# Reordering the input products of the mixers in a two-layer hybrid trunk: an SSD group, two GLA heads, the other SSD group, the other two GLA heads

## The chip, the cores and the metric

The kernel runs on one core of a Trainium2 chip. The metric is the device time in microseconds (us) of one execution. Engines are named as in the profile: PE is the matrix engine (TensorE) and PEld its weight loads, which overlap it; DVE is VectorE, ACT is ScalarE, POOL is GpSimd, SP is SyncE, whose queue carries all the DMAs of the main loop.

## The reference

A trunk of two layers over 512 tokens of width 1024, in float32. Each layer has a mixer and a convolutional feed-forward block (FFN). The mixer projects the normalised tokens once, splits the columns among three sequence mixers, and merges the three results with sigmoid gates:

```python
def mixer_layer(u, w_in, ...):
    proj = u @ w_in                      # 1024 -> all columns below
    (gq, gk, gv, ga, gg, mqk, mv, mi, mf, mo, sz, sxbc, sdt, gates) = jnp.split(proj, ...)
    o_gla = gla(heads(gq, 4), heads(gk, 4), heads(gv, 4), heads(log_a, 4))
    y_gla = group_rmsnorm(o_gla, gla_norm, 4) * jax.nn.silu(gg)
    ...                                  # mlstm: y_m
    xbc = jax.nn.silu(causal_dwconv(sxbc, ssd_conv_w, ssd_conv_b))
    sx, sb, sc = jnp.split(xbc, ...)     # 1024, 2 groups x 128, 2 groups x 128
    y = ssd(heads(sx, 16), dt, a_neg, heads(sb, 2), heads(sc, 2))
    y = (y + ssd_d[:, None] * xh) * jax.nn.silu(sz)
    y_s = group_rmsnorm(y, ssd_norm, 2)
    z = einsum(stack([y_gla, y_m, y_s]), w_branch)
    return sum(sigmoid(gates + gate_b) * z) @ w_out
```

The SSD mixer has two groups of 512 columns of x. Within a group everything depends only on that group's own B, C and x columns (`sb`, `sc`, four tiles of `sx`), up to the gate with `sz` and the root-mean-square norm over the group. The GLA mixer has four heads, each with its q and k (128 columns) and v (256 columns).

## The kernel before, in words

Activations are held transposed: 128 columns by 512 tokens is one tile. A product of one output tile takes 8 slices of the contraction, and each slice three matmuls of 128x128 by 128x512, since weights and activations are split into a high and a low part (`wh`, `wl`, `uh`, `ul`) and the product of the two low parts is left out: 24 matmuls on PE for one output tile, written to one of four PSUM banks called `acc`. For v the operands change places and four `acc` tiles of 512 columns make two heads (`units_tok`). The four other banks are called `m` and serve everything that is no product of a weight: transposes, the scans' small matmuls, states.

Weights come in 512 KB pieces (`raw`, three buffers) by SP's queue; ACT rounds a piece to its high part (`wh`), DVE subtracts to get the low one (`wl`), and two buffers of each hold what PE reads, in units of two output tiles. DVE takes a finished bank out (as `cx`, `gq`, `gk`, `sz` or `G`) and, for SSD, runs a convolution of four taps on it (`cc`).

The table `MIX` lists the columns of the input projection in the order in which they are multiplied, and `layer()` walks it in the same order, with a closure for each tile that says what to do with the bank. The order before is the small columns (`S`), the first SSD group (`sb`, `sc`, four of x), the second SSD group, two GLA heads (q, k, q, k and then four tiles of v), two more GLA heads, the eight `sz` tiles, then gates, branch products and the mLSTM. Numbered from 0, a layer's tiles are 0 to 12 for SSD, 13 to 28 for GLA, 29 to 36 for `sz`.

The sequence mixers run in the background, as generators in `bg`: after each unit of two output tiles `bg` advances each of them by one step, so that their matmuls come between products. `rows` makes the decay rows, `ssd_group(g)` the states and the outputs `sy[4g]` to `sy[4g+3]` of a group, `gla_head(h)` a head, `fin_s(g)` the norm of an SSD group. `bg.drain(condition)` steps the generators until the condition holds. A step of `ssd_group`, called a mix below, takes a pair of decay tiles `bc` and an `eb`, which SP fetches from a scratch in DRAM (`dr`) by three or four DMAs, lets DVE and ACT turn them into matrices, and has PE multiply them by `xd`, the transposed and scaled x. The order in which a group of instructions stands on each engine is chosen by a scheduler when the kernel is built, from the program's order and from priorities, so that moving a tile in `MIX` moves the rows of all the queues.

`fin_s(g)` waits for the last `sz` tile of its group, sums the squares over the columns on PE (`m<-cst,sq`), gets variance and inverse root on DVE in small steps (`svar`, `srt`, `sr`; the line that adds them up is L935), has PE spread the result over the partitions (`rr`, `m<-cst,sr`), and multiplies the four `y` tiles (L238), which are then the activations (`yh`, `yl`) of the first branch product.

Of the kernel before, what the change touches and what calls it, by code (L numbers as in the profile page):

```python
# [53 lines left out]
MIX = ["S"]  # L54
for _g in range(2):
    MIX += [("sxbc", 1024 + 128 * _g), ("sxbc", 1280 + 128 * _g)]
    MIX += [("sxbc", 512 * _g + 128 * _i) for _i in range(4)]
NSSD = len(MIX)

TOK = []  # L60
for _h in range(0, 4, 2):
    MIX += [("gq", 128 * _h), ("gk", 128 * _h), ("gq", 128 * _h + 128), ("gk", 128 * _h + 128)]
    TOK.append(len(MIX))
    MIX += [("gv", 256 * _h + 128 * _i) for _i in range(4)]
# [10 lines left out]
for _h in range(0, 4, 2):  # L75
    MIX += [("mqk", 128 * _h), ("mqk", 512 + 128 * _h), ("mqk", 128 * _h + 128), ("mqk", 640 + 128 * _h)]
    TOK.append(len(MIX))
    MIX += [("mv", 256 * _h + 128 * _i) for _i in range(4)]
# [55 lines left out]
class Kern:  # L134
    def __init__(self, ctx, tc, xT, w8, w11, par, wa, cst, out):
# [44 lines left out]
        for l in range(L):  # L180
            i = 0
            while i < NMIX:
                if i in TOK:
                    self.chunks += [(2, l * N8 + i, k, 2) for k in range(2)]
                    i += 4
                    continue
                n = 1 if i == NSSD - 1 else 2
                self.chunks.append((0, l * N8 + i, KT, n))
# [683 lines left out]
    def layer(self, l):  # L872
        nc = self.nc
        bg = self.bg
# [12 lines left out]
        full = lambda xs: all(x is not None for x in xs)  # L887
        u = self.u


        def evx(i, store, j):
            def ev(ps):
                store[j] = self.silu2(*self.conv(ps, 4, "scw", i, 12, "scb", i))
            return ev
        evs = [lambda ps: bg.add(self.rows(ps))]
        for g in range(2):
            evs += [evx(8 + g, self.sb, g), evx(10 + g, self.sc, g)]
            evs += [evx(4 * g + i, self.sx, 4 * g + i) for i in range(4)]
        bg.add(self.ssd_group(0))
        bg.add(self.ssd_group(1))  # L900
        for i in range(0, NSSD, 2):
            self.wide = i < WIDE
            self.units(u, evs[i:i + 2], boundary=(i == 0), mid=(self.norm_end, self.norm_rows_of_cols))


        for h in range(4):
            def evq(ps):
                self.gq[h] = self.t("gq")
                with self.tc.high_priority(EV_PRIO):
                    self.stt(self.gq[h], ps, 128.0 ** -0.5, self.rstd, ALU.mult, ALU.mult)  # L910

            def evk(ps):
                self.gk[h] = self.t("gk")
                self.first(self.gk[h], ps)
            self.units(u, [evq, evk])
            if h % 2:
                for i in (h - 1, h):
                    self.gv[i] = Blocks([self.v() for _ in range(2)])
                self.units_tok(u, lambda b, ps: self.evac_tok(b, ps, self.gv[h - 1:h + 1]))
        bg.drain(lambda: full(self.sy))  # L920


        rsum_g = self.t("rsg")
        bg.add(self.stagger([self.gla_head(h, rsum_g) for h in range(4)], GLA_LAG))
        sqs, ready, ys, done_s = [None, None], [], [], []

        def fin_s(g):
            while g not in ready:
                yield
            for _ in range(SQY):  # L930
                yield
            ps = self.mps()
            self.colsum(ps, 0, sqs[g])
            var, r = self.small([P, NB], "svar"), self.small([P, NB], "sr")
            nc.vector.tensor_scalar(var, ps[:, 0:NB], 1.0 / 512, 4 * EPS, op0=ALU.mult, op1=ALU.add)  # L935
            with self.tc.high_priority(EV_PRIO):
                self.rsqrt(r, var, self.small([P, NB], "srt"))
            yield
            rr = self.rows_of_cols(r)
            for j in range(4 * g, 4 * g + 4):  # L940
                y = self.sy[j]
                self.stt(y, y, self.col("sn", j), rr, ALU.mult, ALU.mult)
                ys.append(self.split_tile(y))
                self.sy[j] = None
                if j % 2:
                    yield
            if g == 1:
                done_s.append(ys)
        bg.add(fin_s(0))
        bg.add(fin_s(1))  # L950
        for g in range(2):
            for i in range(2):
                def evz(ps, j):
                    s = self.t("sz")
                    self.first(s, ps)
                    s = self.silu2(s)
                    y = self.sy[j]
                    self.mul(y, y, s)
                    q = self.t("sq")
                    self.act(q, y, AF.Square)  # L960
                    if sqs[g] is not None:
                        self.tt(q, q, sqs[g], ALU.add)
                    sqs[g] = q
                    if j % 4 == 3:
                        ready.append(g)
                j = 4 * g + 2 * i
                self.units(u, [lambda ps: evz(ps, j), lambda ps: evz(ps, j + 1)])
# [280 lines left out]
GLA_LAG = 2  # L1248
# [3 lines left out]
WIDE = 2  # L1252
# [97 lines left out]
```

## Time and profile before

| | |
|---|---|
| time, median of 3 runs | 2295.11 us (2294.96 to 2295.38) |
| the profiled execution | 2295.16 us, of which 2293.3 us are the span |
| PE busy | 2279.3 us, 99% of the span |
| PE weight loads | 1876.8 us, 82% |
| DVE busy | 1434.1 us, 63% |
| ACT busy | 902.7 us, 39% |

The time of the profiled execution is the span plus 1.9 us around it. A share of busy time is a mean over the span; the chain that ended last tells which engine's work the end depended on, and idle time of PE, by what ended it, tells how much of the span another order could give back.

### The profile page before, as it was taken

The numbers are of one execution on the slowest core, as the hardware profiler recorded it, in microseconds if no ns is written. First come the engines' busy times: TensorE is split into PE (matmuls) and PEld (weight loads), VectorE is DVE, ScalarE is ACT, GpSimd is POOL, SyncE is SP. The second block draws the span as 40 slices with busy tenths as digits, with TensorE's granted clock in tenths as the row PEclk, the third lists the DMA queues.
The fourth block names the chain that finished last, engine by engine and source line by source line (L and its number), as shares of the span: only waits on it lengthen the run. The fifth ranks groups of instructions, "written<-read, shape, count | busy, mean of one in ns | idle before, by whom it ended". The sixth has DMA issues, their size and how long they took to land.

```text
span 2293.3 us, 27258 instructions
## 1 busy us (share of the span) xinstructions
PE 2279.3 (99%) x10832; PEld 1876.8 (82%) x10832; DVE 1434.1 (63%) x2165; ACT 902.7 (39%) x1344; POOL 2.8 (0%) x22
## 2 busy tenths in 40 slices
PE   9999999999999999999999999999999999999998
PEld 6878888888888888888888788888888888888887
DVE  6966745474464587467579767345744645873774
ACT  6534632333333344234354346233333433442432
POOL 0000000000000000000000000000000000000000
PEclk9999999999999999999999999999999999999999
DMA  5253223332232333232323522232322343232222
GB/s 181 85 156 101 74 74 104 99 120 93 87 111 97 129 100 107 82 101 97 128 85 102 162 92 74 77 107 93 129 90 90 101 132 107 93 97 94 94 91 75
DMA packets 78911, 235.73 MB, mean 103 GB/s; under 512 B 8872, under 2 KB 12264, under 8 KB 78784
## 3 DMA queue, kind: packets, MB, share of 16 engines
q1 hardware_dynamic: 78784, 233.99, 31.7%
q8 instruction: 85, 1.39, 0.3%
q14 instruction: 42, 0.34, 0.1%
HBM read 229.55 MB, written 4.41 MB: 102 GB/s over the span
## 4 chain that ended last, share of the span: by engine, by line
PE 93%; DVE 4%; ACT 2%; issue 1%; DMA 1%; SPq 0%; DVEq 0%; ACTq 0%
PE acc L241 65%; PE m L241 27%; DVE cc L238 1%; PE m L244 1%; ACT la L229 1%; DVE wl L232 1%; DVE la L610 0%; DMA h<-in_xT 0%; DVE og L232 0%; DVE cx L232 0%; DMA dn<-ry 0%; ACT zg L229 0%; ACT cc L229 0%; DVE zg L238 0%; ACT wh L229 0%
## 5 line engine op out<-in xcount | busy, mean ns | idle before, releaser
L229 ACT ACTIVATE wh<-raw 128x1024 fp32r<-128x1024 f32 (+2 forms) x372 | 385.1, 1077 | 586.1 <-PE acc L241 250.9
L241 PE MATMUL acc<-uh,wh 128*128 128x512 f32 x1552 | 609.3, 393 | 2.0 <-DVE mo L232 1.0
L241 PE MATMUL acc<-uh,wl 128*128 128x512 f32 x1552 | 605.9, 391 | 0.4 <-DVE wl L232 0.3
L241 PE MATMUL acc<-ul,wh 128*128 128x512 f32 x1552 | 605.7, 390 | 0.1
L232 DVE TENSOR_TENSOR wl<-raw,wh 128x1024 fp32r<-128x1024 f32 (+2 forms) x372 | 453.2, 1250 | 154.4 <-ACT wh L229 154.0
L241 PEld LDWEIGHTS acc<-uh,wh 128*128 128x128 f32 x1552 | 291.4, 188 | 64.2 <-issue 2.7
L241 PEld LDWEIGHTS acc<-uh,wl 128*128 128x128 f32 x1552 | 291.4, 188 | 62.7 <-DVE wl L232 1.5
L241 PEld LDWEIGHTS acc<-ul,wh 128*128 128x128 f32 x1552 | 291.4, 188 | 61.6 <-DVE ul L238 1.6
L238 DVE SCALAR_TENSOR_TENSOR cc<-cx,par,cc 128x510 f32<-128x510 f32 (+2 forms) x296 | 217.6, 748 | 41.0 <-ACT cc L229 36.9
L241 PE MATMUL acc<-yl,wh 128*128 128x512 f32 x512 | 200.0, 391 | 0.0
L241 PE MATMUL acc<-yh,wl 128*128 128x512 f32 x512 | 199.7, 390 | 0.0
L241 PE MATMUL acc<-yh,wh 128*128 128x512 f32 x512 | 199.6, 392 | 0.0
L241 PE MATMUL m<-uh,wh 128*128 128x512 f32 x384 | 149.8, 390 | 1.2 <-ACT wh L229 1.2
L241 PE MATMUL m<-uh,wl 128*128 128x512 f32 x384 | 149.9, 390 | 0.0
L241 PE MATMUL m<-ul,wh 128*128 128x512 f32 x384 | 149.4, 389 | 0.0
L229 ACT ACTIVATE cc<-cx,par 128x512 f32<-128x512 f32 x128 | 102.8, 809 | 86.6 <-DVE cx L232 86.5
L241 PE MATMUL m<-ah,wl 128*128 128x512 f32 x308 | 120.0, 390 | 0.0
L241 PE MATMUL m<-al,wh 128*128 128x512 f32 x308 | 119.8, 389 | 0.0
L241 PE MATMUL m<-ah,wh 128*128 128x512 f32 x308 | 119.5, 389 | 0.0
L241 PEld LDWEIGHTS acc<-yh,wl 128*128 128x128 f32 x512 | 96.1, 188 | 20.5 <-issue 0.4
L241 PEld LDWEIGHTS acc<-yh,wh 128*128 128x128 f32 x512 | 96.1, 188 | 19.8 <-DVE gg L232 0.4
L241 PEld LDWEIGHTS acc<-yl,wh 128*128 128x128 f32 x512 | 96.2, 188 | 19.5
(204 smaller groups left out, 2653.3 us busy)
## 6 DMA issues: line engine op xcount, KB each, us to landing
raw<-in_w SPq DMA_DIRECT2D x336, 512.0 KB, 3.6
raw<-in_w SPq DMA_DIRECT2D x32, 704.0 KB, 4.0
bc<-dr SPq DMA_DIRECT2D x48, 256.0 KB, 3.6
h<-in_xT SPq DMA_DIRECT2D x16, 256.0 KB, 6.6
eb<-dr SPq DMA_DIRECT2D x32, 128.0 KB, 4.5
bc<-dn SPq DMA_DIRECT2D x16, 256.0 KB, 3.1
kept<-h SPq DMA_DIRECT2D x8, 256.0 KB, 2.0
h<-kept SPq DMA_DIRECT2D x8, 256.0 KB, 5.6
```

Of the source, the lines that this page charges most:

```text
L229: return self.nc.scalar.activation(out, in_, func, bias=bias, scale=scale)
L232: return self.nc.vector.tensor_tensor(out, a, b, op=op)
L238: return self.nc.vector.scalar_tensor_tensor(out, a, s, b, op0=op0, op1=op1)
L241: return self.nc.tensor.matmul(out, lhsT, rhs, start=start, stop=stop)
L244: return self.nc.tensor.transpose(out, x, self.ident)
```

## The change

The table now puts GLA heads 0 and 1 between the two SSD groups, and heads 2 and 3 behind the second. Numbered from 0 the order is `S`, first SSD group (tiles 0 to 6), GLA heads 0 and 1 (7 to 14), second SSD group (15 to 20), GLA heads 2 and 3 (21 to 28), then `sz` as before. Before the gates of the first SSD group only its own four outputs are waited for (`sy[:4]`); the second group's are waited for before its own gates, and the four GLA heads join the background there, two units (four `sz` tiles) later than before. `NSSD`, the number of tiles in the part that is chunked without the pairs, now is 7 and not 13. The matmuls, their number and the buffers are the same; no line of a mixer changes.

```diff
@@ -55,10 +55,11 @@
 for _g in range(2):
     MIX += [("sxbc", 1024 + 128 * _g), ("sxbc", 1280 + 128 * _g)]
     MIX += [("sxbc", 512 * _g + 128 * _i) for _i in range(4)]
-NSSD = len(MIX)
-
-TOK = []
-for _h in range(0, 4, 2):
+    if _g == 0:
+        NSSD = len(MIX)
+
+        TOK = []
+    _h = 2 * _g
     MIX += [("gq", 128 * _h), ("gk", 128 * _h), ("gq", 128 * _h + 128), ("gk", 128 * _h + 128)]
     TOK.append(len(MIX))
     MIX += [("gv", 256 * _h + 128 * _i) for _i in range(4)]
@@ -892,18 +893,22 @@
             def ev(ps):
                 store[j] = self.silu2(*self.conv(ps, 4, "scw", i, 12, "scb", i))
             return ev
-        evs = [lambda ps: bg.add(self.rows(ps))]
-        for g in range(2):
+        bg.add(self.ssd_group(0))
+        bg.add(self.ssd_group(1))
+
+        def ssd_proj(g):
+            evs = [] if g else [lambda ps: bg.add(self.rows(ps))]
             evs += [evx(8 + g, self.sb, g), evx(10 + g, self.sc, g)]
             evs += [evx(4 * g + i, self.sx, 4 * g + i) for i in range(4)]
-        bg.add(self.ssd_group(0))
-        bg.add(self.ssd_group(1))
-        for i in range(0, NSSD, 2):
-            self.wide = i < WIDE
-            self.units(u, evs[i:i + 2], boundary=(i == 0), mid=(self.norm_end, self.norm_rows_of_cols))
+            for i in range(0, len(evs), 2):
+                self.wide = g == 0 and i < WIDE
+                first = g == 0 and i == 0
+                self.units(u, evs[i:i + 2], boundary=first, mid=(self.norm_end, self.norm_rows_of_cols))
 
 
         for h in range(4):
+            if h % 2 == 0:
+                ssd_proj(h // 2)
             def evq(ps):
                 self.gq[h] = self.t("gq")
                 with self.tc.high_priority(EV_PRIO):
@@ -917,11 +922,10 @@
                 for i in (h - 1, h):
                     self.gv[i] = Blocks([self.v() for _ in range(2)])
                 self.units_tok(u, lambda b, ps: self.evac_tok(b, ps, self.gv[h - 1:h + 1]))
-        bg.drain(lambda: full(self.sy))
+        bg.drain(lambda: full(self.sy[:4]))
 
 
         rsum_g = self.t("rsg")
-        bg.add(self.stagger([self.gla_head(h, rsum_g) for h in range(4)], GLA_LAG))
         sqs, ready, ys, done_s = [None, None], [], [], []
 
         def fin_s(g):
@@ -949,6 +953,9 @@
         bg.add(fin_s(0))
         bg.add(fin_s(1))
         for g in range(2):
+            if g == 1:
+                bg.drain(lambda: full(self.sy[4:]))
+                bg.add(self.stagger([self.gla_head(h, rsum_g) for h in range(4)], GLA_LAG))
             for i in range(2):
                 def evz(ps, j):
                     s = self.t("sz")
```

Line numbers of the changed kernel are one higher from the table on; so L238 of before is L239 there, and L271 is L272.

On SP's queue in the first layer, where the last DMAs of the mixes stand among the weight pieces (`raw`), the order before has weight pieces between the two `bc` of one mix.

```order
L845 DMA eb_221_1393<-dr_674 64x512
L502 DMA bc_1494<-dr_674 128x512
L502 DMA bc_1502<-dr_674 128x512
L844 DMA eb_237_1510<-dr_674 64x512
L845 DMA eb_237_1510<-dr_674 64x512
L271 DMA raw_1698<-in_w 128x1024
L502 DMA bc_1513<-dr_674 128x512
L271 DMA raw_1728<-in_w 128x1024
L502 DMA bc_1521<-dr_674 128x512
L844 DMA eb_240_1529<-dr_674 64x512
L845 DMA eb_240_1529<-dr_674 64x512
L271 DMA raw_1762<-in_w 128x1024
```

In the changed kernel the four mixes of the second group come one after the other (`bc_1422`, `bc_1491`, `bc_1611`, `bc_1711`), and this is the stretch with the second and the third of them.

```order
L845 DMA eb_225_1438<-dr_655 64x512
L846 DMA eb_225_1438<-dr_655 64x512
L503 DMA bc_1491<-dr_655 128x512
L503 DMA bc_1499<-dr_655 128x512
L845 DMA eb_235_1507<-dr_655 64x512
L846 DMA eb_235_1507<-dr_655 64x512
L503 DMA bc_1611<-dr_655 128x512
L503 DMA bc_1619<-dr_655 128x512
L845 DMA eb_255_1627<-dr_655 64x512
L846 DMA eb_255_1627<-dr_655 64x512
L272 DMA raw_1709<-in_w 128x1024
L272 DMA raw_1760<-in_w 128x1024
```

So the mixes of the second group follow one another with nothing of the first group between them, and a weight piece, `raw_1709`, stands behind the first three of them on the queue.

On DVE, where the norm of the second SSD group (`svar` to the last `sr`) leads to the first branch product in the first layer, the order before has the small steps on end, with one `G` bank taken out near their end.

```order
L935 TENSOR_SCALAR svar_2379<-m_2374 128x4
L474 TENSOR_SCALAR sr_2380<-svar_2379 128x4
L232 TENSOR_TENSOR srt_2382<-svar_2379,sr_2380 128x4
L238 SCALAR_TENSOR_TENSOR srt_2382<-srt_2382,sr_2380 128x4
L238 SCALAR_TENSOR_TENSOR sr_2380<-srt_2382,sr_2380 128x4
L232 TENSOR_TENSOR srt_2382<-svar_2379,sr_2380 128x4
L238 SCALAR_TENSOR_TENSOR srt_2382<-srt_2382,sr_2380 128x4
L238 SCALAR_TENSOR_TENSOR sr_2380<-srt_2382,sr_2380 128x4
L232 TENSOR_TENSOR srt_2382<-svar_2379,sr_2380 128x4
L238 SCALAR_TENSOR_TENSOR srt_2382<-srt_2382,sr_2380 128x4
L232 TENSOR_TENSOR G_2458<-acc_2433,rstd_263 128x512
L238 SCALAR_TENSOR_TENSOR sr_2380<-srt_2382,sr_2380 128x4
```

The changed kernel has three `ge` multiplications and three `gnb` of GLA heads, and two weight splits (`wl`), between the small steps; the first rows of the chain, from `svar_2244` on, stand just before these.

```order
L233 TENSOR_TENSOR srt_2247<-svar_2244,sr_2245 128x4
L233 TENSOR_TENSOR ge_2195<-ge_2195,gk_690 128x384
L623 TENSOR_SCALAR gnb_2500<-la_283 128x4
L624 TENSOR_SCALAR gnb_2500<-la_283 128x4
L625 TENSOR_SCALAR gnb_2500<-la_283 128x4
L239 SCALAR_TENSOR_TENSOR srt_2247<-srt_2247,sr_2245 128x4
L239 SCALAR_TENSOR_TENSOR sr_2245<-srt_2247,sr_2245 128x4
L233 TENSOR_TENSOR srt_2247<-svar_2244,sr_2245 128x4
L233 TENSOR_TENSOR wl_2556<-raw_2309,wh_2555 128x8x128
L239 SCALAR_TENSOR_TENSOR srt_2247<-srt_2247,sr_2245 128x4
L233 TENSOR_TENSOR wl_2556<-raw_2398,wh_2555 128x8x128
L239 SCALAR_TENSOR_TENSOR sr_2245<-srt_2247,sr_2245 128x4
```

So there is work of a GLA head and of the weights' pipeline inside a chain on which PE's `rr` hangs, where there was only one bank to take out.

On DVE in the first layer, where the fourth tile from the start of the banks' second turn is taken out, the order before has the bank of tile 7 (`cx_563`, x's B column of the second group) behind two rows of `rows`.

```order
L232 TENSOR_TENSOR ra_532<-ig_528,bt_526 32x512
L232 TENSOR_TENSOR r_92_536<-bt_526,mm_530 32x512
L232 TENSOR_TENSOR cx_563<-acc_538,rstd_263 128x512
L238 SCALAR_TENSOR_TENSOR cc_510<-cx_508,par_82,cc_510 128x509
L232 TENSOR_TENSOR wl_719<-raw_574,wh_718 128x1024
```

In the changed kernel the bank of tile 7 is that of GLA's first q.

```order
L239 SCALAR_TENSOR_TENSOR cc_432<-cx_430,par_82,cc_432 128x509
L233 TENSOR_TENSOR r_91_532<-bt_522,mm_526 32x512
L239 SCALAR_TENSOR_TENSOR gq_563<-acc_538,rstd_263 128x512
L233 TENSOR_TENSOR gk_596<-acc_571,rstd_263 128x512
L233 TENSOR_TENSOR ra_528<-ig_524,bt_522 32x512
```

The place has become `gq_563`, with a row of `rows` and a tap of a convolution ahead of it, and the `gk` bank follows at once.

## Rows read from the trace of the kernel before

**Rows 1.** The page, busy time of each engine; chain that ended last.

```profile
PE 2279.3 (99%) x10832; PEld 1876.8 (82%) x10832; DVE 1434.1 (63%) x2165; ACT 902.7 (39%) x1344; POOL 2.8 (0%) x22
...
PE 93%; DVE 4%; ACT 2%; issue 1%; DMA 1%; SPq 0%; DVEq 0%; ACTq 0%
```

**Rows 2.** Waits of PE: line, releaser, us in total, times, longest.

```profile
PE acc L241 <- DVE cx L232: 0.5, 1, 0.5
```

**Rows 3.** Windows: stretch, length, busy us (instructions) of PE, PEld, DVE, ACT, POOL.

```profile
20.00:335.00 315.00, 314.48 (x1612) 256.75 (x1611) 228.62 (x440) 149.68 (x255) 0.82 (x8) 1.00 0.32 101
1155.00:1475.00 320.00, 319.66 (x1645) 262.52 (x1644) 226.87 (x437) 150.06 (x255) 0.82 (x8) 1.00 0.31 98
315.00:490.00 175.00, 175.00 (x774) 144.90 (x773) 89.02 (x110) 55.41 (x74) 0.00 (x0) 1.00 0.30 97
```

**Rows 4.** Chain that ended last, in order of time: start, us, work.

```profile
313.89 179.75 PE acc L241 x792
```

**Rows 5.** Timeline of PE around one pair of mixes between products.

```profile
147.31 0.39 PE L241 MATMUL acc<-uh,wl 128*128 128x512 f32 x1
147.63 0.43 PE L241 MATMUL m<-bc,xd 128*64 128x128 f32 x2
...
151.78 0.47 PE L241 MATMUL acc<-uh,wh 128*128 128x512 f32 x1
152.10 0.39 PE L241 MATMUL acc<-ul,wh 128*128 128x512 f32 x1
```

**Rows 6.** Windows of 22 us in the first layer's SSD and GLA products.

```profile
93.00:115.00 22.00, 22.00 (x118) 18.58 (x117) 21.90 (x57) 5.39 (x10) 0.00 (x0) 1.00 0.32 100
115.00:137.00 22.00, 22.00 (x90) 16.17 (x89) 13.69 (x37) 4.59 (x8) 0.00 (x0) 1.00 0.31 99
```

**Rows 7.** Timeline of DVE where tile 7's bank is taken out.

```profile
75.06 0.69 DVE L232 TENSOR_TENSOR cx<-acc,rstd 128x512 f32<-128x512 f32 x1
75.67 0.74 DVE L238 SCALAR_TENSOR_TENSOR cc<-cx,par,cc 128x509 f32<-128x509 f32 x1
```

**Rows 8.** DVE by shape, 49 to 180 us: count, busy us, mean ns, idle before.

```profile
L232 DVE TENSOR_TENSOR wl<-raw,wh 128x1024 fp32r<-128x1024 f32 x21 | 25.1, 1222 | 0.5 <-ACT wh L229 0.5
L837 DVE TENSOR_SCALAR bc<-bc,ca 128x128 f32<-128x128 f32 x48 | 10.4, 283 | 4.9 <-DMA bc<-dr 4.9
L232 DVE TENSOR_TENSOR xd<-m,cb 128x128 f32<-128x128 f32 x32 | 8.7, 287 | 5.1 <-PE m L244 5.1
...
L238 DVE SCALAR_TENSOR_TENSOR cc<-cx,par,cc 128x511 f32<-128x511 f32 x9 | 6.7, 743 | 0.0
```

**Rows 9.** Tile bc, 130 to 210 us: durations, waits before it, landing.

```profile
L229 ACT ACTIVATE bc<-bc x16: 622/632/641, 139.5 to 188.9; 128x512 f32<-128x512 f32 x16
...
  DMA bc<-dr: 5.8, 5
...
DMA to landing us min/median/max: 3.5/3.7/4.4
```

**Rows 10.** Timeline of DVE, norm of the second SSD group, first layer.

```profile
279.30 0.16 DVE L935 TENSOR_SCALAR svar<-m 128x4 f32<-128x4 f32 x1 [2.80 <-PE m L241]
...
281.76 0.15 DVE L238 SCALAR_TENSOR_TENSOR sr<-srt,sr 128x4 f32<-128x4 f32 x1
...
283.49 0.56 DVE L232 TENSOR_TENSOR ge<-ge,gk 128x384 f32<-128x384 f32 x1 [0.75 <-ACT ge L229]
```

**Rows 11.** Timeline of PE, the same norm.

```profile
278.32 0.95 PE L241 MATMUL m<-cst,sq 128*128 128x1 f32 x8
...
281.22 1.46 PE L241 MATMUL m<-v,kt 128*128 128x256 f32 x6
282.33 0.58 PE L241 MATMUL acc<-uh,wh 128*128 128x512 f32 x1
...
286.64 0.60 PE L244 MATMUL m<-cst,sr 128*128 128x128 f32 x4
...
289.78 0.47 PE L241 MATMUL acc<-yh,wh 128*128 128x512 f32 x1
```

## The prediction, on record before the run

> **What bounds the kernel now.** I read the page first: PE is busy for 2279.3 us of a span of 2293.3 us, and the chain that ended last lies on PE for 93% [rows 1]. A busy PE may still be a PE that works slowly, so I looked at the pace. One run of 792 products on the chain took 179.75 us [rows 4], 226.96 ns each, or 5.45 us for an output tile of 24. That pace is the same wherever products follow each other, so a shorter time must come from fewer matmuls, or from idle time of PE.
>
> The Trainium skill, page "Perfetto Trace Analysis", section "Identifying the Most-Contended Engine", says that the busy share of matmuls is a poor measure of PE and that the one of the weight loads is better. By that sentence 18% of PE would be free here. The stretch with nothing but products has the same 83% of weight loads (144.90 of 175.00 us) with PE never idle [rows 3], so here the figure is the share of the load in the pitch of a product, and no order of the same products changes it.
>
> Idle time of PE is listed by what ended it: eight single waits in the whole span, the one in the reordered tiles of the first layer being 0.5 us for `cx` [rows 2]. The windows give it in one number for each layer: over the input products, from the small columns to the mLSTM's first heads, PE idles for 0.52 of 315 us and for 0.34 of 320 us [rows 3]. So both layers together hold 0.86 us that an order of these tiles can give back. All other waits lie at the layers' beginnings and in the mLSTM and FFN, where the two kernels have the same rows.
>
> DVE is no bound on average (63% [rows 1]), yet it has a regime: through the SSD convolutions it is 21.90 us busy of 22, and over the next 22 us, with v products, only 13.69 [rows 6]. The change puts the lighter stretch between two heavier ones. That would help if PE waited for DVE there; the waits say 0.5 us.
>
> **The change part by part.** The sum is made against the profiled execution, 2295.16 us, which stands 0.05 us above the median of the three runs.
>
> *Products and background matmuls.* Their number is the same, so they give 0. What moves is how often PE goes over from products to background matmuls and back. Around a pair of mixes the start of the first mix comes 0.32 us behind the last product, and the second product behind the mixes 0.32 us after the first [rows 5]; a plain pitch is 0.227 us, so a run of background work costs 0.09 us at its entry and 0.09 at its exit, if neither would be there anyway. By the orders on PE there are 110 such runs before and 120 after. Ten runs by 0.09 to 0.18 us are +0.9 to +1.8 us. I take +0.9, since short runs (four transposes) show the exit alone.
>
> *The one wait in the stretch.* PE waits 0.5 us for `cx` [rows 2]: the bank of tile 7, taken out by DVE from 75.06 us for 0.69 us [rows 7]. In the new order the same place of DVE holds `gq_563`, with as many rows of `rows` and of the convolution ahead of it, and the next user of the bank is v's first tile, again four tiles behind. So the wait stays or goes: between -0.5 and 0, and I take 0.
>
> *DVE over the second group.* In the new order there are 112 instructions of DVE between taking out the first tile of the second group and taking out q of GLA head 2. By the means of [rows 8] (9 `wl` at 1.222, 18 taps at 0.743, 24 `bc` at 0.283, 35 `xd` and `xw` at 0.287, 24 of 512 columns at about 0.69, two of 384 columns) they last 58.9 us; successive ones overlap by some 0.08 us (0.69 long, next one 0.61 later [rows 7]), which leaves 49.9 us. PE passes from the one to the other tile in 144 products, 32.7 us, and background matmuls of about 4.8 us: 37.5 us. DVE so falls back by 12.4 us. PE needs the bank that is taken out last only three tiles later, 16.3 us. A margin of 3.9 us remains, and the background matmuls among these tiles widen it. I take 0; if DVE enters the stretch more than 3.9 us behind, the excess is paid in each layer.
>
> *The mixes of the second group.* Before, the two groups' mixes alternate on SP; now the second group's follow each other, and each needs its `bc` tiles to be freed by an earlier one. From the mix that frees a slot (the third of the first group) to the first of the second group PE has 32 products, 7.26 us, and one mix of about 2.1 us (two mixes take 147.63 to 151.78 us [rows 5]): 9.3 us. What must happen in that time is a landing of 3.7 us, then four `bc` additions, `exp` and a multiplication, for two tiles one behind the other on DVE and ACT: 0.8 + 0.6 + 0.7 for each (four `bc` at 0.283 less their overlap [rows 8], 0.632 for `exp` [rows 9], and 0.69 for a multiplication of 512 columns as that of [rows 7]), partly in parallel, about 4 us. That is 7.7 of 9.3 us, and a margin of 1.6 us. In the trace of before DVE waits 5.8 us for such DMAs, five times [rows 9], and PE, in 315 us with 0.52 us idle for `cx`, waits for no mix [rows 2, 3]. I take 0, with the margin as the smallest of the change. The weight piece behind these DMAs on SP, `raw_1709`, is needed for tile 32, while the third mix's slots are free by tile 27 or 28: four tiles, over 20 us, less 3.7 of landing and under 5 of splitting, so this wait of the queue is covered.
>
> *The GLA heads start later.* Four `sz` tiles later, their matmuls now lie among the last `sz`, the gates and the branch products. They are done before the gates of GLA in both, and from the mLSTM's first products on the orders are alike. 0.
>
> *The norm of the second SSD group.* Before, the sums start on PE at 278.32 us, and `rr` is on PE at 286.64 [rows 11], when `sr` was there since about 281.9 [rows 10]: 4.7 us of cover. Now PE has, between the sums and `rr`, a tile of 24 products, 5.45 us, and three state matmuls of 0.185 (six from 281.22 to the next row at 282.33 [rows 11]): 6.0 us, 6.2 with the entry and exit. DVE has between `svar` and the last `sr` the ten small steps (2.5 us from 279.30 to 281.76 with a `G` of 0.6 among them [rows 10], so 2.0), three `ge` (0.6, 0.6, 0.5 by pitch), three `gnb` (0.1 each) and two `wl` of 1.14 by pitch: 6.3 us, and up to 7.2 with durations in place of pitches. PE waits 0.1 to 1.0 us in each layer; I take 0.3 in each, +0.6, nearer to the lower end since the pitch is what a queue shows. Both ends, +0.2 and +2.0 (and 0, should PE's own background be longer), go into the range. Behind `rr` four `y` multiplications and their splits come before the products that use them; before, that took 3.1 us, 286.64 to 289.78 [rows 11], without a wait, and now some 2.6 us of GLA matmuls lie there, so up to 0.5 us could be missing in each layer; I take 0, since before, too, it waited for nothing.
>
> **Sum.** 2295.16 + 0.9 (runs) + 0.6 (norm) + 0 for all else = 2296.7 us, +0.07%. About 0.2%, 4.6 us, is what a measurement of this kernel can tell from no change, so this is no change.
>
> **The rivals.** *A, my forecast:* PE goes on at its pace and everything moved stays covered, 2294.5 to 2298.5 us.
>
> *B, slower, by mixes or banks of the second group.* The margin of a mix is 1.6 us and DVE is 12.4 us behind at that time. If DVE's work ahead makes the `bc` tiles late by more than 1.6 us, PE stands at each mix with products queued behind it, as its queue is in order. One microsecond of lateness at each of four mixes in two layers is +8 us: 2304 us. The point from which it decides is a lateness of 0.5 us beyond the margin. For it speaks that DVE already waits for `bc` [rows 9], against it that the same waits of DVE reached PE nowhere in that layer before [rows 2, 3].
>
> *C, slower, by the norm.* If a `ge` in the middle of the chain waits for ACT, as one did for 0.75 us [rows 10], or the weight split ahead waits for its piece, the small steps behind it wait too. Three microseconds late in each layer are +6 us: 2302 us.
>
> *D, faster, by mixing regimes.* Light and heavy stretches of DVE alternate, so the waits in them go. All waits there are 0.86 us [rows 3]: 2294.3 us at the best, which is still within 0.2%. The Trainium skill, page "Perfetto Trace Analysis", section "Optimization Strategy", speaks for it: a kernel whose most contended engine changes from regime to regime may gain from interleaving them. By that sentence the order would gain; the trace has the regimes on DVE, but PE is full in both of them [rows 6].
>
> *E, that it does nothing* falls together with A.
>
> **How the numbers follow.** A has 0.80, since the waits of PE in the whole stretch are 0.86 us and each moved piece has a margin or a bounded price. B has 0.08, C 0.07. D has 0.05, and only a gain outside of what the trace shows (more than 4.6 us) would count as faster; of D and such surprises I give 0.04 to faster and put the rest to the same. The predicted time is A's, 2296.7 us. The range goes from 2294.0 (D's full gain with no cost) up to 2301.5, which takes in the bounds of both waits (runs +1.8, norm +2.0, taking the sum to 2299.0) and a slower rival at a third of its price and leaves out less than 2 in 10. Faster 0.04, same 0.81, slower 0.15.
>
> **What would show each step right or wrong.** In the changed kernel's trace: PE's waits list no `bc`, `xd` or `G` with more than 1 us (else B), and `m<-cst,sr` of the second SSD group has at most 1.0 us of idle before it in each layer (else C). PE's busy time is within 2 us of 2279.3. The wait for `cx` of 0.5 us reads `gq` or is gone. DVE's windows of 22 us show a light one between two heavy ones. The prediction would be wrong if PE stands in front of a mix of the second group, or if a piece of work that I counted as covered, such as the `raw` behind the mixes on SP, comes late for the `sz` tiles.

## The result: slower by 0.68%

| | before | changed |
|---|---|---|
| median | 2295.24 us | 2310.9 us (2310.18 to 2312.6, 4 runs) |
| ratio, 95% interval | | 1.0068 [1.005, 1.0085] |
| span of the profiled execution | 2293.3 us | 2310.8 us |
| PE busy | 2279.3 us | 2284.0 us |

The forecast was 2296.7 us and no change, with a range up to 2301.5; the time lies outside of it. The profiled execution is the slowest of the four, 17.5 us longer than that of before. PE is idle for 26.8 us of the span where it was idle for 14.0, and busy for 4.7 us more.

The page of the changed kernel, busy times:

```profile
PE 2284.0 (99%) x10832; PEld 1877.5 (81%) x10832; DVE 1435.0 (62%) x2165; ACT 904.8 (39%) x1344; POOL 2.8 (0%) x22
```

The waits of PE in the changed kernel (line, releaser, us in total, times, longest), the first four and the eighth; [rows 2] has the one for `cx` before:

```profile
PE m L245 <- DVE cc L239: 8.5, 5, 2.8
PE acc L242 <- DVE cx L233: 2.1, 2, 1.1
PE acc L242 <- DVE mo L233: 1.8, 2, 1.5
PE acc L242 <- DVE gq L239: 1.5, 1, 1.5
...
PE m L242 <- DVE xd L233: 0.6, 1, 0.6
```

Its windows over the input products of both layers, which answer to [rows 3]:

```profile
20.00:335.00 315.00, 307.74 (x1570) 251.15 (x1569) 226.13 (x437) 148.18 (x252) 0.82 (x8) 0.99 0.32 100
1155.00:1475.00 320.00, 314.28 (x1603) 255.95 (x1602) 227.50 (x437) 149.62 (x253) 0.72 (x7) 1.00 0.32 99
```

PE idles for 7.3 and 5.7 us where it idled for 0.5 and 0.3. The chief wait is a new one: `m L245 <- DVE cc` is PE in front of the transposes of a convolved x tile of the second SSD group (`m<-cst,cc`), and none of the waits is for a mix. Two windows of the first layer, to be read with [rows 6], show that DVE is not short of time in a plain sense:

```profile
137.00:159.00 22.00, 19.12 (x101) 15.48 (x100) 15.51 (x37) 7.43 (x9) 0.00 (x0) 1.00 0.36 110
159.00:181.00 22.00, 19.15 (x100) 13.95 (x98) 18.96 (x45) 5.94 (x8) 0.00 (x0) 0.92 0.35 107
```

PE waits for DVE in the first of them, and DVE is busy for 15.51 of 22 us in it. So DVE itself waits. The timeline of DVE there (start, us, instruction, and the idle time before it with what ended it):

```profile
139.67 2.36 DVE L233 TENSOR_TENSOR wl<-raw,wh 128x1024 fp32r<-128x1024 f32 x2 [3.18 <-ACT wh L230]
141.95 0.28 DVE L233 TENSOR_TENSOR xd<-m,cb 128x128 f32<-128x128 f32 x1
...
143.14 0.68 DVE L233 TENSOR_TENSOR cx<-acc,rstd 128x512 f32<-128x512 f32 x1
...
149.34 0.87 DVE L838 TENSOR_SCALAR bc<-bc,ca 128x128 f32<-128x128 f32 x4 [3.10 <-DMA bc<-dr]
...
152.17 0.68 DVE L239 SCALAR_TENSOR_TENSOR cc<-cx,cc 128x512 f32<-128x512 f32 x1
...
154.51 0.28 DVE L233 TENSOR_TENSOR xd<-m,cb 128x128 f32<-128x128 f32 x1
154.72 0.68 DVE L233 TENSOR_TENSOR cx<-acc,rstd 128x512 f32<-128x512 f32 x1
...
162.17 0.69 DVE L239 SCALAR_TENSOR_TENSOR cc<-cx,cc 128x512 f32<-128x512 f32 x1 [0.76 <-ACT cx L230]
163.67 0.29 DVE L233 TENSOR_TENSOR xd<-m,cb 128x128 f32<-128x128 f32 x1 [0.81 <-PE m L245]
163.88 0.68 DVE L233 TENSOR_TENSOR cx<-acc,rstd 128x512 f32<-128x512 f32 x1
```

And PE's waits at the same place:

```profile
141.10 0.60 PE L245 MATMUL m<-cst,cc 128*128 128x128 f32 x4
...
152.91 0.66 PE L245 MATMUL m<-cst,cc 128*128 128x128 f32 x4 [2.79 <-DVE cc L239]
...
163.01 0.63 PE L245 MATMUL m<-cst,cc 128*128 128x128 f32 x4 [1.77 <-DVE cc L239]
164.71 0.47 PE L242 MATMUL acc<-uh,wh 128*128 128x512 f32 x1 [1.07 <-DVE cx L233]
```

The two timelines have to be read together, as a ring. PE transposes tile n (163.01). Only then can DVE's `xd` of tile n run (163.67), and the bank of the next tile, `cx`, stands behind that first `xd` on DVE (163.88), though PE had finished that bank long before. Its taps follow, its `cc`, and for that `cc` PE waits with the next transposes. The idle time of DVE ahead of the first wait does not carry the ring's name: the two long stretches, 3.18 and 3.10 us, were ended by ACT's `wh` and by the DMA of `bc`, and none by PE. But the `xd` behind that `wl` pair ran at 141.95 us, and the transposes that they read ended at 141.70 (141.10 and 0.60), so that without the `wl` they could have come 0.25 us earlier at most, and the bank behind them with them. In the order of before, DVE takes out all banks of the second group (tiles 7 to 12) ahead of its first `xd`, so the ring does not exist; the last of these banks and that `xd` stand so on its timeline:

```profile
100.75 0.68 DVE L232 TENSOR_TENSOR cx<-acc,rstd 128x512 f32<-128x512 f32 x1
...
101.94 0.29 DVE L232 TENSOR_TENSOR xd<-m,cb 128x128 f32<-128x128 f32 x1
```

The order on DVE in the first layer of the changed kernel has it three times; here is the middle one, `cx_1193` being the bank of tile 19:

```
L233 TENSOR_TENSOR xd_1160<-m_1155,cb_697 128x128
L233 TENSOR_TENSOR cx_1193<-acc_1168,rstd_263 128x512
L233 TENSOR_TENSOR xw_1082<-m_1155,cb_697 128x128
L233 TENSOR_TENSOR xd_1160<-m_1155,cb_697 128x128
```

`m_1155` are the transposes that stand on PE ahead of tile 23. So the bank of tile 19 is taken out when PE has done tile 22 and all four banks are full. A tile later, with the bank of tile 20, PE waits for it: the 1.07 us for `cx` at 164.71.

There is a second candidate in the same rows: the 3.10 us for which DVE waits for `bc` at 149.34, with the last tap of a second-group tile and its `cc` behind it. SP's queue shows why `bc` is late, with the three weight pieces ahead of it held for 11 us until a buffer is free:

```profile
131.16 11.27 SPq L268 DMA_DIRECT2D raw<-in_w  x3
142.52 0.89 SPq L503 DMA_DIRECT2D bc<-dr  x2
```

The chain that ended last goes by this DMA to the first wait:

```profile
142.52 6.79 DMA bc<-dr
```

A part of the time is no wait. Behind the three waits of the first layer PE's granted clock fell to 0.54 of full speed, near the lower of its two levels (1.2 and 2.4 GHz), for 3.5 us (PE, PEld, DVE, ACT, POOL, then the clock):

```profile
164.70:165.90 1.20, 1.19 (x5) 1.02 (x6) 1.20 (x7) 0.77 (x1) 0.00 (x0) 0.91 0.50 142
165.90:169.40 3.50, 3.50 (x11) 2.70 (x10) 3.50 (x12) 1.28 (x3) 0.00 (x0) 0.54 0.00 0
```

On the chain the 24 products from 164.71 us took 7.32 us, where 24 take 5.45 at the pace of [rows 4]: 1.9 us more. In the second layer, with waits of 1.38, 1.75 and 1.07 us, the clock stayed at 1.00.

### The profile page after: what moved, and what is told of

Read it like the earlier page. It is cut to its first block, busy times and chain, and to the rows that moved or that the text cites. A ratio compares the mean times of both kernels' runs of the same rounds, so it can differ in the third digit from the quotient of the medians.

```text
span 2310.8 us, 27267 instructions
## 1 busy us (share of the span) xinstructions
PE 2284.0 (99%) x10832; PEld 1877.5 (81%) x10832; DVE 1435.0 (62%) x2165; ACT 904.8 (39%) x1344; POOL 2.8 (0%) x22
## 4 chain that ended last, share of the span: by engine, by line
PE 93%; DVE 4%; DMA 1%; issue 1%; ACT 1%; SPq 0%; DVEq 0%; ACTq 0%
PE acc L242 65%; PE m L242 27%; PE m L245 1%; DVE wl L233 1%; DMA bc<-dr 1%; DVE cc L239 1%; DVE og L233 0%; DMA dn<-ry 0%; DMA bc<-dn 0%; DMA h<-in_xT 0%; ACT wh L230 0%; DVE la L611 0%; DVE og L239 0%; DVE bc L838 0%; DVE xd L233 0%
## 5 line engine op out<-in xcount | busy, mean ns | idle before, releaser
L239 DVE SCALAR_TENSOR_TENSOR cc<-cx,par,cc 128x510 f32<-128x510 f32 (+2 forms) x296 | 218.8, 747 | 44.1 <-ACT cc L230 39.8
```

The costliest lines, as they stand in the source:

```text
L239: return self.nc.vector.scalar_tensor_tensor(out, a, s, b, op0=op0, op1=op1)
```

## The experiments

Four theories were on trial. Q: `bc` is late behind the weights on SP. L: DVE has too much to do at this place. G: the later start of the GLA heads. R: the ring. Two more, W and T, stand with the runs that tried them. Most edits also move rows on other queues, since the scheduler places them anew; where that bears on the reading, it is said. All runs of an experiment stand beside runs of the kernel before on the same chip.

**Only one half of the change at a time.** The order with the old rule behind it:

```diff
-        bg.drain(lambda: full(self.sy[:4]))
+        bg.drain(lambda: full(self.sy))
+        bg.add(self.stagger([self.gla_head(h, rsum_g) for h in range(4)], GLA_LAG))
...
-            if g == 1:
-                bg.drain(lambda: full(self.sy[4:]))
-                bg.add(self.stagger([self.gla_head(h, rsum_g) for h in range(4)], GLA_LAG))
```

> The changed order of the products, but with the old rule behind them: all eight outputs of both SSD groups are waited for before the first gates, and the GLA heads start there, as before the change. Theory Q (queue: the decay rows bc stand on SP behind weight pieces that wait for their buffers, DVE waits for them with convolution taps behind, PE waits for the taps): all of the loss comes from the order, 2308 to 2312 us, with the same 8 us or so of PE waits for cc. Theory L (load: DVE simply has too much to do over the second group): the same, 2308 to 2312. Theory G (the later start of the GLA heads costs): 2295 to 2303.

Measured: 2308.65 us, ratio 1.0063 [1.0048, 1.0078]. Its waits of PE begin:

```profile
PE m L245 <- DVE cc L239: 8.5, 5, 3.5
PE acc L242 <- DVE cx L233: 2.1, 2, 1.1
PE acc L242 <- DVE gq L239: 1.5, 1, 1.5
```

The other half, in the kernel before:

```diff
-        bg.drain(lambda: full(self.sy))
+        bg.drain(lambda: full(self.sy[:4]))
-        bg.add(self.stagger([self.gla_head(h, rsum_g) for h in range(4)], GLA_LAG))
...
+            if g == 1:
+                bg.drain(lambda: full(self.sy[4:]))
+                bg.add(self.stagger([self.gla_head(h, rsum_g) for h in range(4)], GLA_LAG))
```

> The order of before, with only the new rule: the gates of the first SSD group wait for that group alone, and the GLA heads start two units later. Theories Q and L: no effect, 2294 to 2297 us. Theory G: 2303 to 2311.

Measured: 2296.14 us, 1.0005 [0.9996, 1.0014]. G is out: the loss is the order's, with the same 8.5 and 2.1 us of waits.

**The mixes' DMAs on another queue.** In the changed kernel and, as the price of the queue, in that of before:

```diff
-                e = self.bcast(dr[16 + hd:17 + hd])
+                e = self.bcast(dr[16 + hd:17 + hd], q=nc.gpsimd)
...
-            self.dq.dma_start(e2[0:64], dr[32 + hd:33 + hd].partition_broadcast(64))
-            self.dq.dma_start(e2[64:128], dr[33 + hd:34 + hd].partition_broadcast(64))
+            nc.gpsimd.dma_start(e2[0:64], dr[32 + hd:33 + hd].partition_broadcast(64))
+            nc.gpsimd.dma_start(e2[64:128], dr[33 + hd:34 + hd].partition_broadcast(64))
```

> The changed kernel, with the DMAs of the SSD mixes (bc and eb) issued from POOL's queue, which has no weights on it, in place of SP's. Theory Q: DVE's wait of 3.1 and 1.7 us for bc goes, the PE waits for cc fall from 8.5 us to under 2, and the time to 2296 to 2301 us (the 1.5 us wait for gq and some transitions stay). Theory L: DVE has the same work, so the waits for cc stay at 6 us or more and the time at 2308 to 2312.

> The kernel before, with the same DMAs on POOL's queue: what the other queue costs or gives by itself. Theory Q: PE waited for no mix before, so nothing changes, 2294 to 2297 us. If issuing from POOL has a price of its own, it shows here as more than 2297.

Measured: 2309.21 us, 1.0064 [1.0047, 1.0081], and in the kernel before 2298.05 us, 1.0013 [1.0003, 1.0022]. In the first PE waits less for `cc`, but as long for `cx`:

```profile
PE m L245 <- DVE cc L239: 4.6, 2, 2.3
PE acc L242 <- DVE cx L233: 2.1, 2, 1.1
```

On its DVE timeline there is no wait ahead of the `bc` that had 3.10 us:

```profile
146.84 1.66 DVE L838 TENSOR_SCALAR bc<-bc,ca 128x128 f32<-128x128 f32 x8
```

The first wait of each layer (2.79 and 1.38 us) is gone; what is left is 2.31 us of `cc` and 1.07 of `cx` in each. So Q names something real, 3.9 of the 10.6 us of PE's waits, and 6.7 us stay with `bc` early. The time does not weigh Q fairly: the other queue costs 3 us by itself, and PE's granted clock was low for longer than in the changed kernel, which has 0.76 over its worst 7 us in the first layer and 1.00 in the second. Here both layers have such a stretch:

```profile
160.00:167.00 7.00, 5.79 (x16) 4.55 (x17) 6.17 (x20) 2.16 (x4) 1.04 (x2) 0.57 0.14 44
1303.00:1310.00 7.00, 6.07 (x20) 4.86 (x21) 6.96 (x22) 2.49 (x4) 0.65 (x2) 0.76 0.10 37
```

An estimate from these rows (3 us for the queue, 3 for the clock) puts the kernel with `bc` early at some 2303 us, with half of the loss still there.

**Less work for DVE just there.** Two of three taps left out for the second group's x tiles (its convolution has fewer taps than the reference's):

```diff
-                store[j] = self.silu2(*self.conv(ps, 4, "scw", i, 12, "scb", i))
+                store[j] = self.silu2(*self.conv(ps, 2 if 4 <= i < 8 else 4, "scw", i, 12, "scb", i))
```

> The changed kernel with two of the three taps left out in the convolution of the second group's four x tiles, so that DVE has some 5.3 us less to do in each layer just there (8 taps at 0.67 us by pitch); PE's order stays the same but for a few products. Theory L, as it stands after the run with the mixes' DMAs on POOL (DVE takes on the first group's mixes while it convolves the second group, and falls behind PE by four tiles): PE's waits for cc and cx, 10.6 us, fall to under 4, and the time to 2297 to 2303 us. Theory Q (late bc rows set the end): the first wait of each layer, 2.8 and 1.4 us, stays, and the time is 2304 to 2309.

Measured: 2300.41 us, 1.0022 [1.0012, 1.0031]. PE's waits:

```profile
PE acc L242 <- DVE cx L233: 2.1, 2, 1.1
...
PE m L245 <- DVE cc L239: 0.7, 2, 0.3
```

As L expected in time. That Q's first wait is gone says nothing against Q, since the DMAs did not stay where they were: with fewer taps on DVE the first `bc` stands on SP ahead of two of the three weight pieces, and is issued 11 us earlier than in the changed kernel.

```profile
131.40 0.93 SPq L503 DMA_DIRECT2D bc<-dr  x2
```

And a shorter DVE leg shortens a ring too; the waits for `cx` did not move, which fits the ring better.

**The first group's mixes held back.**

```diff
+        while self.sx[7] is None:
+            yield
         q = []
         for i in range(4 + SSD_LEAD):
```

> The changed kernel, with the first group's mixes held back until the second group's last x tile is convolved: the same work and the same order of products, but no mix of the first group lies among the second group's convolutions. Theory L: the waits for cc and cx go (under 2 us in both layers), no row of bc stands before a tap, and the time is 2296 to 2301 us, with the 1.5 us for gq left. If mixes among convolutions are not what DVE lacks time for (theory W: the weight splits, which wait for PE to free their buffers, hold DVE up ahead of the tiles), the waits stay above 6 us and the time is 2306 to 2312.

Measured: 2352.51 us, 1.0248 [1.0231, 1.0265]. A miss in time on both sides; W's waits above 6 us came. The waits at the convolutions do not go, with no mix among them before the last tile, and the mixes, now late, hold DVE ahead of the gates:

```profile
PE acc L242 <- DVE sz L233: 22.7, 6, 5.8
...
PE acc L242 <- DVE cx L233: 4.3, 4, 1.1
PE m L245 <- DVE cc L239: 3.7, 3, 1.4
```

That 8.0 us for `cx` and `cc` remain nearly without the mixes speaks against L in the form that was tried. It is also what led to R: what was left in the rows of DVE between the banks were the `xd`. W got no run of its own; the 0.25 us above bound it at the first of the three places in the changed kernel.

**The transposes a step later.**

```diff
+            if g:
+                yield
             x2 = self.sx[4 * g + i]
             p1 = self.mps()
```

> The changed kernel, with one more step between a convolved x tile of the second group and its transposes on PE, so that PE asks for it a tile later; DVE's work is the same. Theory L: DVE is late by its load, so the wait only moves: the waits for cc shrink by at most half, but those for the banks (cx) grow, 2303 to 2310 us. If only the transposes stand too early on PE (theory T), the waits go and the time is 2296 to 2301 us.

Measured: 2295.97 us, 1.0002 [0.9992, 1.0011]. The whole loss is gone with one added step. PE's waits have no `cc` and no `cx`:

```profile
PE acc L242 <- DVE gq L239: 1.5, 1, 1.5
...
PE m L245 <- DVE sr L239: 1.1, 2, 0.5
```

DVE does the same work, and in 137 to 159 us it is busy for 20.26 of 22 us in place of 15.51. On DVE the banks of tiles 17 and 18 now stand ahead of any `xd` of the second group. On SP the first `bc` has moved ahead of two weight pieces here, too. L's 2303 to 2310 is out; the waits went as T had them.

**The ring cut.** Transposes later also means other rows on PE. So the next run leaves the transposes on PE where they are and cuts the dependence on them: `xd` and `xw` of the second group read the convolved tile itself, and not its transposes, which stay on PE with nothing reading them.

```diff
-                src = p1[:, blk(b)].rearrange("p (h c) -> p h c", h=2)
+                src = (x2 if g else p1)[:, blk(b)].rearrange("p (h c) -> p h c", h=2)
```

> The changed kernel, with xd and xw of the second group read from the convolved tile itself and not from its transposes (so those outputs hold the tile untransposed): the transposes stay on PE where they are, the rows of PE and DVE keep their order and their number, and only DVE's dependence on the transposes is gone. Theory R (a ring: DVE takes out tile n+1 only behind the xd of tile n, the xd wait for transposes on PE, and these for the taps of tile n, so DVE cannot use the time in which PE multiplies): PE's waits for cc and cx fall from 10.6 to under 4 us, and the time to 2297 to 2302 us. Theory L (load alone): DVE does the same work in the same order, so the waits stay above 7 us and the time is 2306 to 2311.

Measured: 2300.66 us, 1.0019 [1.0009, 1.0028]. PE's waits begin:

```profile
PE acc L242 <- DVE mo L233: 1.8, 2, 1.1
PE m L245 <- DVE cc L239: 1.7, 2, 0.8
PE acc L242 <- DVE gq L239: 1.5, 1, 1.5
```

The waits for `cc` and `cx` fall from 10.6 to 1.7 us with the same number of instructions, so L, load alone, is out. On PE the rows keep their order up to the last transposes of the second group in the first layer, so T, their place on PE alone, is out as well. In the window in which DVE was busy for 15.51 us it now is for 19.86:

```profile
137.00:159.00 22.00, 22.00 (x117) 18.08 (x116) 19.86 (x46) 8.63 (x11) 0.00 (x0) 1.00 0.43 130
```

Contrary to the expectation, the rows of DVE and SP did not keep their order. With the dependence gone, the scheduler put the first tile's `xd` and the bank of tile 18 ahead of the two `wl` (this `cx` comes at 137.89 us and not at 143.14), and on SP the first `bc` ahead of two weight pieces, so that DVE has no wait for it:

```profile
131.74 0.93 SPq L503 DMA_DIRECT2D bc<-dr  x2
...
137.89 0.69 DVE L233 TENSOR_TENSOR cx<-acc,rstd 128x512 f32<-128x512 f32 x1
...
143.53 0.87 DVE L838 TENSOR_SCALAR bc<-bc,ca 128x128 f32<-128x128 f32 x4
```

So the run shows what the dependence costs together with the rows that it had forced into place, and not the dependence alone. Of the 8.9 us of waits that go, some may be Q's: the run with `bc` early and the ring whole took 3.9 us away. Whether the late `bc` is itself an effect of the ring no run shows; the `wl` that freed the buffer for the weight piece ahead of it had waited for ACT's `wh` (3.18 us above), and not for an `xd`.

**Two more on the steps.** The one step later with the old rule, and two steps later with the new one:

```diff
+            if g:
+                yield
+                yield
```

> The run with the transposes one step later, but with the old rule behind the products (GLA heads and the waiting for all eight outputs as before the change). Theory R: no wait for cc or cx, and without the later heads the waits for sr (1.1 us in two) go too: 2293 to 2296 us. If the later heads have no price, the same as with them, 2295 to 2297.

> The changed kernel with the second group's transposes two steps later. Theory R: the ring is already open with one step, so a second gives nothing, 2294 to 2298 us; what may come instead is a mix that is late for its gates, since x is scaled later (waits for sz or y, above 2298).

Measured: 2306.2 us, 1.0044 [1.0029, 1.0059], and 2323.29 us, 1.0119 [1.0102, 1.0135]. The first missed; the second missed its 2294 to 2298 and came out by the alternative it names, a late mix, with the waits at the mix itself. The new waits are of the same kind in both, first the one and then the other:

```profile
PE m L242 <- DVE bc L233: 6.0, 5, 1.7
```

```profile
PE m L242 <- DVE bc L233: 15.2, 2, 7.6
```

Later transposes make later mixes. Where the gates then wait for outputs that are not yet there, the mixes are asked for one right behind the other, and PE stands in front of them until DVE has worked `bc` up. The new rule, which asks for the second group's outputs two units later, is worth some 10 us with the transposes a step later (2295.97 against 2306.2), and no difference is shown for it in the orders of before and of the change.

No run beat the kernel before; the best, with one step, equals it.

## Why the prediction was wrong

*What bounds the kernel:* right in the main. Of the 17.5 us by which the profiled span grew, 12.8 are PE's idle time and 4.7 its busy time, in which 1.9 us of a lower clock lie.

*The step that failed* is "DVE over the second group". It let DVE's queue run freely for 49.9 us against PE's 37.5, asked only when the bank that is taken out last is needed again, and found a margin of 3.9 us. Two things in it were wrong. The nearest one who waits for DVE's work is not the user of the bank but the transposes of the convolved tile, which stand on PE three to four tiles behind the tile's products. And DVE does not run freely: its `xd` wait for these transposes, with the next bank queued behind. The order on both engines showed this before the run, `cx` between `xd` on DVE, and a row of before had such a wait, 5.1 us of `xd` for PE's `m` [rows 8], which cost PE nothing there; I had counted the instructions and not followed which of them wait for whom. What the runs put in the place of the 0 is 10.6 us of waits for `cc` and `cx` in both layers, and 1.9 us of a lower clock behind them. Of these 10.6 us, 6.7 stay when `bc` is early and 1.7 when the dependence on the transposes is cut.

*The one wait in the stretch* was mis-sized: the range was -0.5 to 0, and the wait of 0.5 us became one of 1.5 for `gq`. The bank is taken out 0.3 us later, at 75.38 us, and PE came to it earlier, as four small matmuls (`m<-cst,ra`) that stood ahead of it at 74.69 us before were no longer there.

*The transitions* were priced at 0.9, up to 1.8 us. They were not measured alone. PE's busy time grew by 4.7 us, of which the clock takes 1.9, so that at most 2.8 us are left for them. With the transposes a step later PE was busy for 2277.8 us, less than before, so no price of theirs is shown.

*The mixes* were right in that PE waits for none, and their 0 was wrong all the same: DVE's longest wait for `bc` is 3.1 us (in both kernels five such waits have some 6 us together, [rows 9] for before), the taps of a second-group tile stand behind it, and 3.9 us of PE's waits go when it goes. A late `bc` was priced only as PE waiting at a mix. *The later GLA heads* at nothing were right as the run of that half alone shows. *The norm* at 0.1 to 1.0 us for each layer: no such wait in the changed kernel, and 1.1 us in both together when the transposes came later, inside the range.

*The signs.* PE's busy time was to stay within 2 us of 2279.3 and grew by 4.7. The signs on the waits for mixes and for the norm held, and none of the signs named the transposes.

*The rivals.* B had the place and half the size (+8 us, 2304, against +15.7), but with mixes as those who wait. Its point of decision, a margin of 1.6 us on `bc`, decides a part: with `bc` early 6.7 of the 10.6 us of waits stayed. D, that interleaving heavy and light stretches of DVE gives time back, went the other way. The Trainium skill, page "Perfetto Trace Analysis", section "Optimization Strategy", holds such interleaving to be worth a try; here the measurement is 1.0068, and what it cost was the distance between a tile's products and the work that depends on them.

What stays open: the ring with the dependence cut still takes 2300.66 us, 4.8 us more than before on the same chip. The 1.5 us for `gq` and the 1.7 for `cc` are in it, and by the profiled executions PE idles for some 3 us more than before and is busy for 2.5 more; the rest was not taken apart. Nor is it shown how the 10.6 us divide between the late `bc` and the ring: no run cut the one and kept every row of the other in place.

## What to carry to other kernels

When an order is changed on an engine that is nearly full, do not ask only whether the helping engine has time enough; follow the instructions that stand between one bank and the next on it, and ask for each whether it waits for the full engine. If it does, the two engines walk in step and a backlog is never worked off. A helper that is idle in the very window in which it is waited for (15.51 of 22 us busy here) is a reason to look, though the profile may book its idle time to something that stands in front, as it did here. The remedy that gave all of some 15 us back was distance, a step between a result and the work on it that goes back to the first engine; less work on the helper gave two thirds back (2300.41 us). A second step of distance cost 27 us.

## What the runs showed of the hardware

Three waits of 2.79, 1.77 and 1.07 us within 15 us were followed by 3.5 us at a granted clock of 0.54, so that the waits cost a third more than they lasted; the second layer's waits of 1.38, 1.75 and 1.07 us at the same places were not. With the mixes' DMAs on POOL's queue both layers had the same two waits, 2.31 and 1.07 us, and the granted clock was 0.57 over 7 us in the first and 0.76 in the second. Issuing these DMAs from POOL's queue made the kernel before slower by 3 us (1.0013 [1.0003, 1.0022]), with PE as seldom idle as before (14.0 us) and busy for 2.5 us more.
